# Folding the compressed keys and values from high and low parts, and a new order at the end of the cross attention

## The chip, the cores and the metric

The kernel runs on one core of one Trainium2 chip. The metric is the time of one execution on the device, in microseconds (us); several runs are timed, and one more execution is recorded by the hardware profiler. The engines are named as in the profile: PE does the matmuls (PEld loads their stationary operand), DVE is the vector engine, ACT the scalar engine, POOL the GpSimd engine, SP issues most of the DMAs. Every engine works through its own queue in order.

## The reference

The reference is one layer of a decoder trunk: 512 tokens of width 1024, 256 memory tokens. The normalized input `h` is projected once, `z = h @ W_in`, and the columns of `z` go to a pooling mixer (A), a sparse attention (B) and a cross attention into the memory (C); their gated sum goes through `w_o` and is followed by a retrieval over 16384 single-neuron experts and a last norm. What matters here is one piece of B, the compressed keys and values:

```python
cmp_start = jnp.arange(n_cmp) * CMP_STRIDE                # n_cmp = 31, stride 16
tok_idx = cmp_start[:, None] + jnp.arange(CMP_LEN)[None]  # windows of 32 tokens

def compress(tok, pe, w):                                 # tok: (B, T, 4 heads, 64)
    blk = tok[:, tok_idx] + pe[None, None, :, None, :]
    blk = blk.transpose(0, 1, 3, 2, 4).reshape(B, n_cmp, G, CMP_LEN * dh)
    return blk @ w                                        # (32*64) -> 64

kc = compress(k_cmp_tok, pe_k, w_cmp_k)
vc = compress(v_cmp_tok, pe_v, w_cmp_v)
```

`pe` is a learned encoding of the 32 places of a window. The pooling mixer takes, for its group `gr`, a trailing mean over 2, 4, 8 or 16 tokens minus the token, and then a 128x128 matrix of the group.

## The kernel before, in words

All large matmuls are made from split operands. A matrix X becomes a high part, `hi`, in the format fp32r, and a low part, `lo = X - hi`, also fp32r; a product is the sum of `hi*hi`, `lo*hi` and `hi*lo`. The helper `split` makes both parts: ACT copies the source into `hi` (line 144), then DVE (or POOL, for weights) subtracts (line 145).

A **z tile** is 128 columns of `z`, for all 512 tokens: 24 matmuls of 512 columns (line 172), 16 with the high part of the weights and 8 with the low part, into a PSUM bank of the tag `z`. There are two banks of each tag (`z`, `S`, `tr`, `o`), used in turn: a new tile takes the bank of the one before last and waits until that one's last reader is done. The weights come through `Feed`: SP fetches a raw tile `wr`, ACT makes `wh`, POOL makes `wl`. `take` hands out the tile that is due and, right behind it in the queues, has the next one split (`ahead`). So the split of the next z tile's weights stands in ACT's queue after everything that was issued before this `take`, and ahead of what is issued after it.

The stretch that the change touches is written out by hand as a list of steps, `cross_order`. Each step issues its instructions on all engines at once, in the order of the list, so the list is the order of every engine's queue:

- `Z0`..`Z3` (`cross_q`): the z tile of a cross-attention head's queries, then `qh` on ACT and `ql` on DVE.
- `S` (`cross_scores`): 12 matmuls into two banks `S`; for each, DVE takes the maximum (line 475) and ACT two exponentials (line 478).
- `R` (`cross_scale`): DVE, a reciprocal and four scalings (line 487).
- `T` (`cross_turn`): 8 transposes into two banks `tr` (line 496), each split by ACT and DVE into `xPT`.
- `O` (`cross_out`): 6 matmuls (line 508) into a bank `z`, split into `oxh`, `oxl`.
- `P` (`pool_window`): a z tile; POOL clears the margins of `u` and `pacc` (lines 523, 529), ACT copies `z` to `u` (line 524), DVE adds shifted copies (line 530, one to four times, three for `P2`, four for `P3`), forms `pl` (lines 534 to 536), and `pl` is split into `ph`.
- `G` (`pool_group`): the group's matrix on `ph` (3 matmuls into a bank `z`; `G3` comes later, into `S`), then `poolh` on ACT and `pooll` on DVE (lines 544, 545).
- `v00`..`v13` (`values`): the values of the two other branches, 24 matmuls of 280 columns into a bank `o`; ACT and DVE split 256 columns of the bank into `V` (lines 144, 145), and ACT takes the last 24 columns into `gsig` (line 439).
- `k0`, `k1`, `v0`, `v1` (`cmp_z`): a z tile of two heads' keys (values) to be compressed. Four DVE instructions (line 572), one for each head and half window, add the encoding `pe2` and write the sum into `TP`, which is f32 and is so laid out that the place within the half window is a row of its own.
- `kc`, `vc` (`cmp_fold`): 16 matmuls in plain f32 (line 580), 128 weights by 124 columns, into a bank `o`; the profile shows 32 instructions for them, two for each. `kc` is then split into `KC`, `vc` is copied into `vt` (line 587).
- `A`: has the weights of one more z tile split ahead.

Behind the list come the relative bias table (`bias_table`, line 664, `rtab` at line 665), the first z tiles of the sparse attention's keys and queries, and, after the first four chunks of four matmuls of these, `cmp_rows`: four transposes of `vt` (line 592), split into `VC` (lines 144, 145), and copies into `VH` (line 600). `G3` follows three chunks later. From there on the order of the work is as written in other parts of the kernel that the change does not touch.

Of the kernel before, what the change touches and what calls it, by code (L numbers as in the profile page):

```python
# [10 lines left out]
F32 = mybir.dt.float32  # L11
F32R = mybir.dt.float32r
# [3 lines left out]
AF = mybir.ActivationFunctionType  # L16
OP = mybir.AluOpType
# [14 lines left out]
def f(ap):  # L32
    return ap.bitcast(F32)
# [15 lines left out]
def drain(gen):  # L49
    for _ in gen:  # L50
        pass
# [70 lines left out]
def layer(ctx: ExitStack, tc: tile.TileContext, A: dict, out: bass.AP, dbg=None):  # L122
    nc = tc.nc
    v, s, g, pe = nc.vector, nc.scalar, nc.gpsimd, nc.tensor
# [6 lines left out]
    def sbuf(stack, name, side="left"):  # L131
        return stack.enter_context(tc.tile_pool(name=name, bufs=1, side=side, reuse_waits="tile"))

    def psum(tag, shape, bufs=2, dt=F32):
        return ps.tile(shape, dt, tag=tag, name=tag, bufs=bufs)
# [7 lines left out]
    def split(hi, lo, src, eng=None):  # L143
        s.activation(hi, src, AF.Copy)  # L144
        (eng or v).tensor_tensor(lo, src, f(hi), op=OP.subtract)  # L145
# [88 lines left out]
    for vc in range(2):  # L234
        for kq in range(2):
            feed.plan(("mv", vc, kq), A["w_mv"][vc, kq], 4, 256, v if vc else None)
    cross_order = ("Z0 v00 S0 v01 R0 v02 T0 v03 W1 Z1 P0 O0 S1 v10 R1 v11 T1 G0 Z2 P1 O1 S2 v12 R2 v13 T2 G1 "
                   "Z3 P2 O2 A S3 k0 R3 k1 T3 v0 G2 kc O3 v1 P3 vc G3")
    cross_order = cross_order.split()
    for c in cross_order:  # L240
        if c[0] == "Z":
# [46 lines left out]
    pm = gfeed.pool = sbuf(pms, "pm", "right")  # L288
# [103 lines left out]
    def ztile_steps(key, p):  # L392
        yield from mm3_steps(p, feed.take(key), hn, KD)

    def ztile(i):
        p = psum("z", [128, T])
        drain(ztile_steps(("z", i), p))
        return p
# [5 lines left out]
    KC = ap_.tile([128, 4, 2, 32], F32R, name="KC")  # L404
# [50 lines left out]
    def cross_q(hx):  # L455
        p = ztile(20 + hx)
        qh = xw.tile([128, T], F32R, name="qh")
        ql = xw.tile([128, T], F32R, name="ql")
        s.activation(qh, p, AF.Copy, scale=128.0 ** -0.5)
        v.scalar_tensor_tensor(ql, p, 128.0 ** -0.5, f(qh), op0=OP.mult, op1=OP.subtract)  # L460
        XQ[hx] = (qh, ql)
# [19 lines left out]
    def cross_scale(hx):  # L481
        pr, sm = XP[hx]
        v.reciprocal(sm, sm)
        for hq in range(2):
            for q_ in range(2):
                qb = 2 * hq + q_
                v.tensor_scalar(pr[:, qb], pr[:, qb], sm[:, qb:qb + 1], None, op0=OP.mult)
# [61 lines left out]
    cst = ExitStack()  # L549
    C = {}  # L550

    def cmp_open():
        cp = C["cp"] = sbuf(cst, "cp")
        for kv in range(2):
            C["wc", kv] = cp.tile([128, 16, 128], F32, tag="wc", name="wc")
            C["pe2", kv] = cp.tile([128, 2, 16], F32, tag=f"pe2{kv}", name="pe2")
            for a in (0, 64):
                for half in range(2):
                    nc.sync.dma_start(C["pe2", kv][a:a + 64, half], A["pe2"][kv, half * 64:half * 64 + 64])
            if kv == 0:  # L560
                nc.sync.dma_start(C["wc", 0], A["w_cmp"][0])

    def cmp_z(kv, gp_):
        cp = C["cp"]
        if gp_ == 0:
            C["TP", kv] = cp.tile([128, 16, 4, 31], F32, tag="TP", name="TP", bufs=2)
        p = ztile(4 + 2 * kv + gp_)
        for gi in range(2):
            a = gi * 64
            for half in range(2):  # L570
                b = half * 64
                v.tensor_tensor(C["TP", kv][b:b + 64, :, gp_ * 2 + gi],
                                p[a:a + 64, half * 16:half * 16 + 496].rearrange("p (c l) -> p l c", l=16),
                                C["pe2", kv][a:a + 64, half][:, :, None].to_broadcast([64, 16, 31]), op=OP.add)

    def cmp_fold(kv):
        cp, wc, TP = C["cp"], C["wc", kv], C["TP", kv]
        pc = psum("o", [128, 256])
        for l in range(16):
            pe.matmul(pc[:, 0:124], wc[:, l], TP[:, l], start=l == 0, stop=l == 15)  # L580
        pcv = pc[:, 0:124].rearrange("p (g c) -> p g c", c=31)
        if kv == 0:
            nc.sync.dma_start(C["wc", 1], A["w_cmp"][1])
            split(KC[:, :, 0, 0:31], KC[:, :, 1, 0:31], pcv)
        else:
            C["vt"] = pm.tile([64, 4, 31], F32, name="vt")
            v.tensor_copy(C["vt"], pcv[0:64])

    def cmp_rows():
        pt = psum("tr", [128, 4, 128])  # L590
# [14 lines left out]
    for c in cross_order:  # L605
        n = int(c[1]) if c[1:].isdigit() else None
        if c[0] == "Z":
            cross_q(n)
        elif c[0] == "S":
            cross_scores(n)  # L610
        elif c[0] == "R":
            cross_scale(n)
        elif c[0] == "W":
            wv_part(n)
        elif c[0] == "T":
            cross_turn(n)
        elif c[0] == "O":
            cross_out(n)
        elif c[0] == "P":
            pool_window(n)  # L620
            if n == 0:
                gfeed.fetch(1)
                gfeed.part(1)
        elif c == "A":
            feed.fetch(feed.i + 2)
            feed.part(feed.i + 2)
        elif c == "G3":
            pass
        elif c[0] == "G":
            pool_group(n)  # L630
        elif len(c) == 3:
            br, b = int(c[1]), int(c[2])
            values(br, b)
            if (br, b) == (1, 3):
                vst.close()
                v.tensor_scalar(gsig, gsig, 0.5, 0.5, op0=OP.mult, op1=OP.add)
                v.tensor_scalar(gsig[:, 0, 0:16], gsig[:, 0, 0:16], has, None, op0=OP.mult)
                cmp_open()
        elif c == "kc":
            cmp_fold(0)  # L640
        elif c == "vc":
            cmp_fold(1)
        else:
            cmp_z(int(c[0] == "v"), n)
    cst.close()
    xwst.close()
    dump("poolT", f(poolh)); dump("poolL", f(pooll))
# [401 lines left out]
    for at in attention():  # L1049
# [5 lines left out]
        while done < goal:  # L1055
            c = next(filler, None)
# [68 lines left out]
    src = A["iota128"]  # L1125
# [178 lines left out]
    for hp in range(16):  # L1304
        if hp < 15:
            p = psum("z", [128, T])
# [515 lines left out]
def _layout(I):  # L1822
    a = {}
    a["x"] = I["x"][0]
    a["mem"] = I["mem"][0]
    a["rel_bias"] = I["rel_bias"]
    for k in ("g_mix", "g_mem", "g_ffn"):
        a[k] = I[k][0]
    a["g_final"] = I["g_final"]
    w = I["w_in"][0]  # L1830
    o_q, o_kv, o_g, o_x, o_m = 512, 1536, 3072, 3120, 3632
    kvc = [w[:, o_kv + 256 * i:o_kv + 256 * (i + 1)] for i in range(6)]
    q = w[:, o_q:o_kv]
    ks = np.stack([kvc[2].reshape(D, 4, 64), kvc[4].reshape(D, 4, 64)], axis=2).reshape(D, 512)
    zt = np.concatenate([ks, kvc[0], kvc[1], q, w[:, 0:512], w[:, o_x:o_m], w[:, o_m:]], axis=1)
    a["w_z"] = _tiles(zt, 128)
    wv = []
    for i, vv in enumerate((kvc[3], kvc[5])):
        wv.append(_tiles(np.concatenate([vv, w[:, o_g + 24 * i:o_g + 24 * (i + 1)]], axis=1), 280)[0])
    a["w_v"] = np.stack(wv)  # L1840
    wc, pe = [], []
    for kk in ("k", "v"):
        w4 = I["w_cmp_" + kk][0].reshape(2, 16, 64, 64)
        one = w4.transpose(0, 2, 1, 3).reshape(128, 16, 64)
        wc.append(np.concatenate([one, one], axis=2))
        pe.append(I["pe_" + kk][0].reshape(2, 16, 64).transpose(0, 2, 1).reshape(128, 16))
    a["w_cmp"] = np.stack(wc)
    a["pe2"] = np.stack(pe)
    a["w_pool_grp"] = I["w_pool_grp"][0]
    a["pool_scale"] = I["pool_scale"][0].reshape(4, 128).T  # L1850
    a["w_pool_out"] = _tiles(I["w_pool_out"][0], 128)
    a["w_nsa_out"] = _tiles(I["w_nsa_out"][0], 128)
    a["w_x_out"] = _tiles(I["w_x_out"][0], 128)
    mk = I["w_mem_kv"][0]
    a["w_mk"] = _tiles(mk[:, 0:512], 128)
    a["w_mv"] = mk[:, 512:].reshape(2, 4, 128, 2, 256).transpose(3, 0, 2, 1, 4).reshape(2, 2, 128, 1024)
    a["w_o"] = I["w_o"][0].reshape(4, 2, 128, 2, 512).transpose(3, 0, 2, 1, 4).reshape(2, 4, 128, 1024)
    a["w_peer_q"] = _tiles(I["w_peer_q"][0], 128)
    a["sub_keys"] = I["peer_sub_keys"][0].reshape(16, 128, 128).transpose(2, 0, 1)
    u4 = I["peer_u"][0].reshape(128, 128, D)  # L1860
    a["u_t"] = u4.reshape(128, 128, KD, 128).transpose(1, 3, 2, 0).reshape(128, 128, KD * 128)
    a["u_rows"] = u4.transpose(1, 0, 2).reshape(128 * 128, D)
    a["v_rows"] = I["peer_v"][0].reshape(128, 128, D).transpose(1, 0, 2).reshape(128 * 128, D)
    a = {k: np.ascontiguousarray(x) for k, x in a.items()}
    a.update(_consts())
    return a
# [15 lines left out]
```

## Time and profile before

| | |
|---|---|
| median of 3 runs | 1793.06 us (1792.14 to 1795.39) |
| the profiled execution, its own time | 1791.84 us |
| its span, first to last instruction | 1790.1 us |
| PE busy | 1769.6 us, 99% of the span |
| DVE, ACT, POOL busy | 1374.7, 832.8, 855.8 us |
| share of PE in the chain that ended last | 90% |
| the steps `Z3` to `vc` in the trace | from 103.6 to 154.7 us |

The page's busy times say how much of the span an engine had an instruction at work. The chain is followed back from the last instruction, at each step to what released it; its times in order show where PE works without a gap and where another engine holds the end. In a list in order of time, a row has the start, the duration, the engine, the line, the operation, what is written from what, and in brackets how long the engine had been idle and what ended that.

### The profile page before, as it was taken

What the parts mean: (1) busy time and instruction counts of PE and PEld (TensorE: products, weight loads), DVE (VectorE), ACT (ScalarE), POOL (GpSimd) and SP (SyncE); (2) the same over time, 40 slices, a digit from 0 to 9 for tenths busy, and PEclk for the clock granted to TensorE, in tenths of its full rate; (3) what the DMA queues carried; (4) which work ended last, traced back from release to release, by engine and by line L of the source; (5) the groups of instructions that cost most, each with busy time, mean ns of one, the idle gap of its engine ahead of it and who ended that gap; (6) DMA issues with size and microseconds to landing.
All of it is one profiled execution on the core that took longest, in us unless ns stands there. A gap on an engine that the chain in (4) does not pass through costs nothing.

```text
span 1790.1 us, 28200 instructions
## 1 busy us (share of the span) xinstructions
PE 1769.6 (99%) x10114; PEld 1564.2 (87%) x10114; DVE 1374.7 (77%) x2846; ACT 832.8 (47%) x1476; POOL 855.8 (48%) x681
## 2 busy tenths in 40 slices
PE   8999999999999999999999999999999999999998
PEld 7988888888888888999999999999999988888886
DVE  5454147776653369999999976999998999999997
ACT  6434257777642333463555554333333333333334
POOL 3333555556643323434555405666666654444430
PEclk9999999999999999999999999999999999999999
DMA  6225631112123532377999989999999999999993
GB/s 227 90 85 163 218 122 60 49 60 71 60 77 99 187 125 83 114 244 239 360 362 372 374 293 388 410 409 391 381 395 384 366 390 406 408 406 403 398 407 127
DMA packets 155614, 456.55 MB, mean 255 GB/s; under 512 B 16513, under 2 KB 55857, under 8 KB 152786
## 3 DMA queue, kind: packets, MB, share of 16 engines
q1 hardware_dynamic: 80850, 253.10, 38.9%
q0 software_dynamic: 47488, 172.38, 25.0%
q10 hardware_dynamic: 27136, 29.26, 4.9%
q8 instruction: 80, 1.31, 0.3%
q14 instruction: 60, 0.49, 0.1%
HBM read 411.82 MB, written 48.10 MB: 257 GB/s over the span
## 4 chain that ended last, share of the span: by engine, by line
PE 90%; DVE 4%; ACT 3%; DMA 1%; issue 1%; POOL 0%; DVEq 0%; SPq 0%; ACTq 0%; POOLq 0%
PE z L172 47%; PE S L1656 9%; PE tr L1656 9%; PE o L1656 9%; PE S L916 2%; PE tr L948 1%; PE o L964 1%; PE S L1177 1%; PE o L435 1%; PE o L1497 1%; PE S L1497 1%; PE tr L1497 1%; PE o L1261 1%; ACT pr L929 1%; DVE wl L145 0%
## 5 line engine op out<-in xcount | busy, mean ns | idle before, releaser
L144 ACT ACTIVATE wh<-wr 128x1024 fp32r<-128x1024 f32 (+2 forms) x365 | 371.4, 1025 | 140.7 <-PE z L172 45.2
L145 POOL TENSOR_TENSOR wl<-wr,wh 128x1024 fp32r<-128x1024 f32 (+2 forms) x110 | 241.8, 2199 | 320.1 <-ACT wh L144 267.9
L172 PE MATMUL z<-hfh,wh 128*128 128x336 f32 (+1 forms) x1136 | 362.6, 326 | 0.1
L172 PE MATMUL z<-hfl,wh 128*128 128x336 f32 (+1 forms) x1136 | 359.4, 323 | 0.0
L145 DVE TENSOR_TENSOR wl<-wr,wh 128x1024 fp32r<-128x1024 f32 x255 | 306.2, 1216 | 58.4 <-ACT wh L144 56.9
L1520 POOL DMA_INDIRECT ug<-in_v_rows_dram,ids x128 | 178.8, 1397 | 173.4 <-DVE x1g L1540 155.1
L1520 POOL DMA_INDIRECT ug<-in_u_rows_dram,ids x128 | 199.8, 1561 | 92.0 <-DVE ug L1534 74.1
L172 PEld LDWEIGHTS z<-hfh,wh 128*128 128x128 f32 x1136 | 213.3, 188 | 7.6 <-ACT wh L144 1.0
L172 PEld LDWEIGHTS z<-hfl,wh 128*128 128x128 f32 x1136 | 213.4, 188 | 6.5
L172 PE MATMUL z<-hfh,wl 128*128 128x336 f32 (+1 forms) x1136 | 207.1, 324 | 1.1 <-DVE wl L145 1.1
L144 ACT ACTIVATE wgh<-gh 128x384 fp32r<-128x384 f32 x128 | 67.3, 526 | 286.8 <-DVE gh L1635 273.5
L172 PEld LDWEIGHTS z<-hfh,wl 128*128 128x128 f32 x1136 | 182.3, 188 | 7.6 <-DVE wl L145 1.9
L1226 ACT ACTIVATE hg<-z 128x336 f32<-128x336 f32 x128 | 57.7, 451 | 232.8 <-PE z L172 232.6
L1540 DVE SCALAR_TENSOR_TENSOR x1g<-ug,wgt,x1g 128x1024 f32<-128x1024 f32 x128 | 163.9, 1280 | 1.4
L1534 DVE SCALAR_TENSOR_TENSOR ug<-ug,hf 128x1024 f32<-128x1024 f32 x128 | 152.4, 1218 | 5.7 <-DMA ug<-in_u_rows_dram,ids 5.7
L172 PE MATMUL z<-hnh,wh 128*128 128x512 f32 x384 | 150.8, 393 | 0.0
L172 PE MATMUL z<-hnl,wh 128*128 128x512 f32 x384 | 150.2, 391 | 0.0
L1420 POOL DMA_INDIRECT ux<-in_u_rows_dram,idx x48 | 89.6, 1866 | 53.9 <-DVE ux L1428 48.8
L937 POOL TENSOR_SCALAR pr<-pr,sm,gsig 128x128 f32<-128x128 f32 (+3 forms) x128 | 78.5, 617 | 74.6 <-DVE sm L1011 58.3
L952 DVE TENSOR_TENSOR PB<-tr,PB 128x128 fp32r<-128x128 f32 (+3 forms) x128 | 62.5, 488 | 50.5 <-ACT PB L951 50.1
L172 PE MATMUL z<-hnh,wl 128*128 128x512 f32 x384 | 98.8, 392 | 0.0
L145 DVE TENSOR_TENSOR wgl<-gh,wgh 128x384 fp32r<-128x384 f32 x128 | 71.1, 556 | 32.8 <-ACT wgh L144 32.8
(418 smaller groups left out, 3651.1 us busy)
## 6 DMA issues: line engine op xcount, KB each, us to landing
wr<-in_u_t_dram SPq DMA_DIRECT2D x128, 512.0 KB, 6.7
wr<-in_v_rows_dram SPq DMA_DIRECT2D x128, 512.0 KB, 9.8
wr<-in_w_z_dram SPq DMA_DIRECT2D x48, 512.0 KB, 3.6
gd<-stg ACTq DMA_DIRECT2D x11, 2048.0 KB, 16.9
hg<-hd SPq DMA_DIRECT2D x80, 168.0 KB, 10.9
gj<-gd SPq DMA_DIRECT2D x8, 1408.0 KB, 12.5
go<-gd SPq DMA_DIRECT2D x8, 1408.0 KB, 15.1
hd<-hg POOLq DMA_DIRECT2D x66, 168.0 KB, 6.3
```

The source lines that it names most:

```text
L144: s.activation(hi, src, AF.Copy)
L145: (eng or v).tensor_tensor(lo, src, f(hi), op=OP.subtract)
L172: pe.matmul(p, w[a][:, k], xs(x[b], k), start=k == 0 and a == 0 and b == 0, stop=k == nk - 1 and a == 1)
L937: g.tensor_scalar(pr[:, 0:n], pr[:, 0:n], sm, gsig[:, qb, c:c + 1], op0=OP.mult, op1=OP.mult)
L952: return lambda: v.tensor_tensor(lo, pt[:, 0:qb + 1], f(hi), op=OP.subtract)
L1226: s.activation(hg[:, X:], p[:, X:NT], AF.Gelu)
L1420: g.indirect_dma_start(out=XR[k], out_offset=None, in_=A["u_rows"], in_offset=bass.IndirectOffsetOnAxis(ap=idx[:, k:k + 1], axis=0))
L1497: pe.matmul(pg[:, n], oa[:, t_ // 2, :, t_ % 2], ob[:, r, t_ // 2, :, t_ % 2], start=n == 0 and r == 0, stop=n == 3 and r == 1, skip_group ...
L1520: g.indirect_dma_start(out=row, out_offset=None, in_=src, in_offset=bass.IndirectOffsetOnAxis(ap=ids[:, b, k:k + 1], axis=0))
L1534: v.scalar_tensor_tensor(row, row, 1.0, hf[:, b], op0=OP.mult, op1=OP.mult, accum_out=act[:, m:m + 1])
L1540: v.scalar_tensor_tensor(X1[b], rows.pop(m), wgt[:, m - 128:m - 127], X1[b], op0=OP.mult, op1=OP.add)
L1656: pe.matmul(acc_o[2 * b + half], a[:, b * 128:(b + 1) * 128], c[:, half], start=k == 0 and i == 0, stop=k == 127 and i == 2)
```

## The change

Three things are changed, all in this stretch.

The fold is made from parts. The weights `w_cmp` are no longer stored twice side by side; `cmp_load` fetches 64 columns, and `cmp_weights` splits them (ACT, and POOL for the low part) into `wcs`, whose 128 columns are the 64 high and the 64 low ones. `cmp_parts` takes the place of the four additions: it splits the four pieces of the z tile, so that there is an ACT copy and a DVE subtraction for each, into `TP`, now fp32r with 250 columns: 124 high, 124 low, and two more, the encoding's high and low part. So one chain of 16 matmuls of 250 columns yields all products, in two halves of 64 partitions. `cmp_fold` sums them: ACT copies the lower half into `low`, DVE adds the encoding's columns, copies one, and makes two sums of 124 columns into `t_`. For the keys, `KC` is then made of `t_` by two copies on ACT and two subtractions on DVE.

The encoding `pe2` comes in two DMAs in place of eight. The second weights are loaded after `k1` in place of after `kc`, and there is one buffer of `TP` in place of two.

The order is changed: `P2` moves from behind `Z3` to behind `k1`; `k0` comes ahead of `S3`; `kc` moves from behind `G2` to ahead of `v0`.

```diff
-    cross_order = (... "Z3 P2 O2 A S3 k0 R3 k1 T3 v0 G2 kc O3 v1 P3 vc G3")
+    cross_order = (... "Z3 O2 A k0 S3 R3 k1 P2 T3 kc v0 G2 O3 v1 P3 vc G3")

+    def cmp_load(kv):
+        C["raw", kv] = C["cp"].tile([128, 16, 64], F32, name="wc")
+        nc.sync.dma_start(C["raw", kv], A["w_cmp"][kv])
+
+    def cmp_weights(kv):
+        C["wc", kv] = C["cp"].tile([128, 16, 2, 64], F32R, name="wcs")
+        split(C["wc", kv][:, :, 0], C["wc", kv][:, :, 1], C["raw", kv], g)

     def cmp_open():
...
+            C["pe2", kv] = cp.tile([128, 16], F32, tag=f"pe2{kv}", name="pe2")
+            nc.sync.dma_start(C["pe2", kv], A["pe2"][kv])
+        cmp_load(0)

     def cmp_z(kv, gp_):
...
+        C["p", kv, gp_] = ztile(4 + 2 * kv + gp_)
+
+    def cmp_parts(kv, gp_):
+        if gp_ == 0:
+            TP = C["TP", kv] = C["cp"].tile([128, 16, 250], F32R, name="TP")
+            split(TP[:, :, 248], TP[:, :, 249], C["pe2", kv])
+        p, TP = C.pop(("p", kv, gp_)), C["TP", kv]
         for gi in range(2):
+            src = p[gi * 64:gi * 64 + 64]
+            o = (gp_ * 2 + gi) * 31
             for half in range(2):
                 b = half * 64
-                v.tensor_tensor(C["TP", kv][b:b + 64, :, gp_ * 2 + gi], ..., op=OP.add)
+                split(TP[b:b + 64, :, o:o + 31], TP[b:b + 64, :, 124 + o:155 + o],
+                      src[:, half * 16:half * 16 + 496].rearrange("p (c l) -> p l c", l=16))

     def cmp_fold(kv):
...
         for l in range(16):
-            pe.matmul(pc[:, 0:124], wc[:, l], TP[:, l], start=l == 0, stop=l == 15)
+            pe.matmul(pc[:, 0:250], wc[:, l].rearrange("p r d -> p (r d)"), TP[:, l], ...)
+        t_ = pm.tile([64, 4, 31], F32, name="vt")
+        tf = t_.rearrange("p g c -> p (g c)")
+        low = C["cp"].tile([64, 250], F32, name="low")
+        s.activation(low, pc[64:128, 0:250], AF.Copy)
+        v.tensor_tensor(low[:, 248:250], low[:, 248:250], pc[0:64, 248:250], op=OP.add)
+        v.tensor_copy(low[:, 249:250], pc[0:64, 249:250])
+        for i in range(2):
+            v.scalar_tensor_tensor(tf, pc[0:64, i * 124:i * 124 + 124], low[:, 248 + i:249 + i],
+                                   tf if i else low[:, 0:124], op0=OP.add, op1=OP.add)
         if kv == 0:
-            nc.sync.dma_start(C["wc", 1], A["w_cmp"][1])
-            split(KC[:, :, 0, 0:31], KC[:, :, 1, 0:31], pcv)
+            for a in (0, 64):
+                s.activation(KC[a:a + 64, :, 0, 0:31], t_, AF.Copy)
+            for a in (0, 64):
+                v.tensor_tensor(KC[a:a + 64, :, 1, 0:31], t_, f(KC)[0:64, :, 0, 0:31], op=OP.subtract)
         else:
-            C["vt"] = pm.tile([64, 4, 31], F32, name="vt")
-            v.tensor_copy(C["vt"], pcv[0:64])
+            C["vt"] = t_

     # in the loop over cross_order
             cmp_z(int(c[0] == "v"), n)
+            cmp_parts(int(c[0] == "v"), n)
+            if n == 0:
+                cmp_weights(int(c[0] == "v"))
+            if c == "k1":
+                cmp_load(1)
```

More of the change, by code (lines that the diff above doesn't have):

```diff
@@ L237, in layer @@
     cross_order = ("Z0 v00 S0 v01 R0 v02 T0 v03 W1 Z1 P0 O0 S1 v10 R1 v11 T1 G0 Z2 P1 O1 S2 v12 R2 v13 T2 G1 "
-                   "Z3 P2 O2 A S3 k0 R3 k1 T3 v0 G2 kc O3 v1 P3 vc G3")
+                   "Z3 O2 A k0 S3 R3 k1 P2 T3 kc v0 G2 O3 v1 P3 vc G3")
     cross_order = cross_order.split()
@@ L554, in cmp_open @@
         for kv in range(2):
[L555 to L561, printed above, removed]
+            C["pe2", kv] = cp.tile([128, 16], F32, tag=f"pe2{kv}", name="pe2")
@@ L563, in cmp_z @@
+            nc.sync.dma_start(C["pe2", kv], A["pe2"][kv])
+        cmp_load(0)
     def cmp_z(kv, gp_):
-        cp = C["cp"]
+        C["p", kv, gp_] = ztile(4 + 2 * kv + gp_)
+    def cmp_parts(kv, gp_):
         if gp_ == 0:
-            C["TP", kv] = cp.tile([128, 16, 4, 31], F32, tag="TP", name="TP", bufs=2)
-        p = ztile(4 + 2 * kv + gp_)
+            TP = C["TP", kv] = C["cp"].tile([128, 16, 250], F32R, name="TP")
+            split(TP[:, :, 248], TP[:, :, 249], C["pe2", kv])
+        p, TP = C.pop(("p", kv, gp_)), C["TP", kv]
@@ L568, in cmp_z @@
         for gi in range(2):
-            a = gi * 64
+            src = p[gi * 64:gi * 64 + 64]
+            o = (gp_ * 2 + gi) * 31
             for half in range(2):
                 b = half * 64
-                v.tensor_tensor(C["TP", kv][b:b + 64, :, gp_ * 2 + gi],
-                                p[a:a + 64, half * 16:half * 16 + 496].rearrange("p (c l) -> p l c", l=16),
-                                C["pe2", kv][a:a + 64, half][:, :, None].to_broadcast([64, 16, 31]), op=OP.add)
+                split(TP[b:b + 64, :, o:o + 31], TP[b:b + 64, :, 124 + o:155 + o],
+                      src[:, half * 16:half * 16 + 496].rearrange("p (c l) -> p l c", l=16))
@@ L576, in cmp_fold @@
     def cmp_fold(kv):
-        cp, wc, TP = C["cp"], C["wc", kv], C["TP", kv]
+        wc, TP = C["wc", kv], C["TP", kv]
         pc = psum("o", [128, 256])
         for l in range(16):
-            pe.matmul(pc[:, 0:124], wc[:, l], TP[:, l], start=l == 0, stop=l == 15)
-        pcv = pc[:, 0:124].rearrange("p (g c) -> p g c", c=31)
+            pe.matmul(pc[:, 0:250], wc[:, l].rearrange("p r d -> p (r d)"), TP[:, l], start=l == 0, stop=l == 15)
+        t_ = pm.tile([64, 4, 31], F32, name="vt")
@@ L1844, in _layout @@
         one = w4.transpose(0, 2, 1, 3).reshape(128, 16, 64)
-        wc.append(np.concatenate([one, one], axis=2))
+        wc.append(one)
         pe.append(I["pe_" + kk][0].reshape(2, 16, 64).transpose(0, 2, 1).reshape(128, 16))
```

## The prediction

> **What bounds the kernel now.** I read the page first, then the windows of the stretch that the change touches, then the chain that ended last in order of time.
>
> ```profile
> PE 1769.6 (99%) x10114; PEld 1564.2 (87%) x10114; DVE 1374.7 (77%) x2846; ACT 832.8 (47%) x1476; POOL 855.8 (48%) x681
> PE 90%; DVE 4%; ACT 3%; DMA 1%; issue 1%; POOL 0%; DVEq 0%; SPq 0%; ACTq 0%; POOLq 0%
> ```
> ```profile
> 103.00:163.00 60.00, 60.00 (x307) 50.09 (x306) 30.56 (x56) 20.01 (x42) 21.34 (x22) 1.00 0.28 88
> 163.00:222.00 59.00, 59.00 (x262) 48.88 (x261) 8.23 (x12) 22.51 (x32) 29.04 (x25) 1.00 0.72 234
> ```
> ```profile
> 115.98 1.41 PE S L473 x12
> 117.39 10.90 PE z L172 x48
> 128.29 0.87 PE tr L496 x8
> 129.16 6.14 PE z L172 x27
> 135.31 3.57 PE o L580 x32
> 138.88 1.38 PE z L508 x6
> 140.25 10.89 PE z L172 x48
> 151.14 3.57 PE o L580 x32
> 154.71 0.96 PE z L664 x2
> 155.67 3.86 PE z L172 x16
> 159.53 0.34 PE tr L592 x4
> ```
>
> PE is never idle from 103 to 222 us (first number of the windows: length, then PE, PEld, DVE, ACT, POOL busy). So whatever PE saves in the steps up to `vc` comes off the end, and whatever idle time is put between its steps is added: the 59 us behind, gapless too, absorb nothing. ACT is busy 20 of 60 us and DVE 31, but in order; what counts is when, after a z tile, each of them is done with it.
>
> **Part 1: the matmuls of the fold.** 32 instructions take 3.57 us a fold. In their place stand 16 fp32r matmuls of 250 columns. The nearest row are the 12 score matmuls of 256 columns, 1.41 us, 0.1175 each: 16 x 0.1175 = 1.88 us, a gain of 1.69 a fold, **3.4 us** in all. That is also the most that the change can gain. From the other side: fp32r with few columns might run at a quarter of the rate.
>
> ```profile
> L812 PE MATMUL z<-KC,Q x64: 192/277/278, 222.3 to 423.6; 128*128 128x64 f32 x64
> L473 PE MATMUL S<-Kh,qh x16: 279/279/279, 48.6 to 116.9; 128*128 128x256 f32 x16
> ```
>
> 64 columns take as long (277 ns) as 256 (279), which would fit that, at 16 x 0.43 = 6.9 us a fold. But the quickest takes 192 ns, 85 less: one whose weights were loaded before its turn. The others wait for weights, not for columns. I take 1.88.
>
> **Part 2: the splitting, and what orders it.** Before, a z tile to be compressed costs four DVE additions, 2.8 us. Now each piece is an ACT copy and a DVE subtraction, all eight reading one PSUM bank. Does ACT's second copy wait for DVE's first subtraction, though neither needs the other's result? The trace has three places with two engines on one bank.
>
> ```profile
> 100.82 0.42 DVE L145 TENSOR_TENSOR V<-o,V 128x256 fp32r<-128x256 f32 x1 [1.74 <-ACT V L144]
> 101.28 0.19 ACT L439 ACTIVATE gsig<-o 128x24 f32<-128x24 f32 x1 [0.49 <-DVE V L145]
> 160.15 0.21 DVE L145 TENSOR_TENSOR VC<-tr,VC 31x64 fp32r<-31x64 f32 x1 [1.88 <-ACT VC L144]
> 160.39 0.21 ACT L144 ACTIVATE VC<-tr 31x64 fp32r<-31x64 f32 x1 [0.28 <-DVE VC L145]
> 160.64 0.21 DVE L145 TENSOR_TENSOR VC<-tr,VC 31x64 fp32r<-31x64 f32 x1 [0.28 <-ACT VC L144]
> 169.24 1.20 ACT L744 ACTIVATE Q<-z 64x512 fp32r<-64x512 f32 x2
> 170.47 1.39 DVE L749 SCALAR_TENSOR_TENSOR Q<-z,Q 64x512 fp32r<-64x512 f32 x2 [3.35 <-ACT Q L744]
> ```
>
> `gsig` reads other columns of the bank than DVE's subtraction does and needs nothing from it, yet starts 0.04 us after its end. The four splits of `VC` out of one bank go strictly in turn, 0.49 us each for two instructions of 0.21. And the first subtraction of `Q` needs only the first copy (partitions 0 to 63), but starts 0.03 after the second (partitions 64 to 127) ended. So accesses of two engines to one PSUM tile stand in the program's order here, whichever part they read. The change issues copy, subtraction, copy, subtraction, where `Q` issues both copies first.
>
> ```profile
> 163.88 0.57 ACT L716 ACTIVATE KK<-z 64x512 fp32r<-64x512 f32 x1
> L572 DVE TENSOR_TENSOR TP<-z,pe x16: 666/673/679, 122.9 to 147.8; 64x496 f32<-64x496 f32 x16
> ```
>
> One turn is 0.58 + 0.04 + 0.67 + 0.04 = 1.33 us; four, begun 0.2 after the tile's end, are done **5.5 us** after it (without that order 3.6: copies 0.5 apart, subtractions 0.7), and both ACT and DVE are held for that long. Encoding columns (0.2 on each engine) and `cmp_weights` (ACT 1.05, POOL 2.4) ride along.
>
> **Part 3: the new order, walked through.** Durations not shown yet:
>
> ```profile
> 109.91 0.69 DVE L460 SCALAR_TENSOR_TENSOR ql<-z,qh 128x512 fp32r<-128x512 f32 x1 [4.31 <-ACT qh L459]
> 121.41 0.47 ACT L478 ACTIVATE xpr<-S,xnm 128x256 f32<-128x256 f32 x1 [0.52 <-DVE xnm L475]
> 120.70 1.28 DVE L475 TENSOR_REDUCE xnm<-S 128x2 f32<-128x512 f32 x2
> 123.23 1.07 ACT L144 ACTIVATE wh<-wr 128x1024 fp32r<-128x1024 f32 x1
> 124.38 2.40 POOL L145 TENSOR_TENSOR wl<-wr,wh 128x1024 fp32r<-128x1024 f32 x1 [1.00 <-ACT wh L144]
> 114.74 0.60 ACT L524 ACTIVATE u<-z 128x512 f32<-128x512 f32 x1 [3.92 <-PE z L172]
> 118.82 0.63 ACT L144 ACTIVATE ph<-pl 128x512 fp32r<-128x512 f32 x1 [3.48 <-DVE pl L536]
> 128.76 1.09 ACT L144 ACTIVATE xPT<-tr 128x512 fp32r<-128x512 f32 x2 [4.47 <-PE tr L496]
> 134.66 2.78 DVE L572 TENSOR_TENSOR TP<-z,pe 64x496 f32<-64x496 f32 x4 [2.28 <-PE z L172]
> 137.47 0.75 DVE L545 SCALAR_TENSOR_TENSOR pooll<-z,scl,poolh 128x512 fp32r<-128x512 f32 x1
> 157.39 0.28 DVE L587 COPY vt<-o 64x124 f32<-64x124 f32 x1
> ```
>
> `k0` needs `Z3`'s bank; `qh` (0.60, as `u`) and `ql` free it 1.65 us after `Z3` with their hand-overs, and only `O2`, 1.36, lies between: **0.3** idle. Now count from `k0`'s end. `k0`'s turns hold DVE to 5.5, the maxima of `S3` follow to 6.8, its four exponentials (0.47 each) to 8.1, and only then comes `wh` for `P2` in ACT's queue: ready at 9.2. PE has had `S3` (1.41) and `k1` (5.45) and wants `P2` at 6.9: **2.4** idle. `P2` ends at 14.7. `k1`'s turns run on ACT from 9.05 to 13.6, then `wh` for `v0`, and POOL's `wl` to 17.1; the clearing of `u` stands behind that, so ACT's `u` starts at 17.3 in place of 14.9. From `u` to `ph` the trace has 4.1 us: `ph` at 21.4, and the copies for `T3` behind it to 23.0, `low` of `kc` to 23.3, four DVE additions behind DVE's part of `T3` to 24.9, `KC` to 25.5, `wh` for `v1` to 26.5, the encoding 0.2: only at 26.7 do `v0`'s turns begin, done at 32.0. PE meanwhile: `T3` 0.87, `kc` 1.88, `v0` 5.45, `G2` 0.68, at 23.6. `O3` takes the bank of the z tile before last, `v0`'s, and must wait for its last subtraction: **8.5** idle. Before, `kc` stood between, 3.57 us of cover, and the bank was free at 137.44, ahead of `O3` at 138.88.
>
> Smaller ones: `v1` needs `G2`'s bank, whose `poolh` (0.7) and `pooll` (0.75) now come behind `v0`'s turns, 0.6. `vc` needs `v1`'s turns (5.5, cover `P3` 5.45), 0.2. Behind `v1`'s turns stand `wh` and `wl` of the next weights, (ACT free 0.7 ahead of `P3`'s end, then 1.05 and 2.4), so `u` of `P3` starts 3.0 after `P3`'s end, not 0.2; the first key tile needs that bank, 0.7. Then `vt`: `u` at 3.0, 4.9 to `ph` (one addition more than `P2`), 0.63 and 0.69 for its split with `low` beside it, and the sums, two as long as `vt`'s copy and two narrow ones, 1.0 as an estimate: 10.3 after `P3`. PE reaches line 592 after `vc`, the bias table, and 3.64 of the key tile, 7.3 after `P3`: **3.1** idle. Before, `vt` was one copy, at 157.7, 1.8 ahead.
>
> **Part 4: PE's clock after the long gap.**
>
> ```profile
> 7.50 1.97 PE L203 MATMUL tr<-ident,hb 128*128 128x128 f32 x8 [1.38 <-DVE hb L324]
> 14.22 1.27 PE L203 MATMUL tr<-ident,hb 128*128 128x128 f32 x8
> 1775.00:1790.00 15.00, 8.14 (x35) 6.14 (x34) 9.85 (x20) 5.79 (x17) 0.00 (x0) 0.86 0.29 106
> ```
>
> The first 16 transposes, over some 3.4 us from 7.5, go at about half the pace of those at 14.2, and in the last 15 us, where PE idles, the granted clock is 0.86 (the number ahead of the last two). After 8.5 us of idleness I expect `O3` and a little of `v1` at half pace: at most 1.7, at least nothing; 0.6 is covered by `v1`'s own wait. I take 1.2.
>
> **At nothing** I put the DMAs: two of `pe2` in place of eight, a smaller `w_cmp` fetched some 20 us ahead; the second one waits on SP for POOL's low part of the first, done 8.3 after `k0`, ahead of the next fetch; uncovered, it would hold up the fetch for `v1`, wanted at 25.5. `G2` finds `ph` ready 0.1 early.
>
> **The sum.** Idle 0.3 + 2.4 + 8.5 + 0.6 + 0.2 + 0.7 + 3.1 = 15.8, less 3.4, plus 1.2: **+13.6** on the profiled execution's 1791.84 us. The median of the runs is 1793.06, 1.2 above it, so 1806.7; the chained waits lean to the long side, and I say **1806 us**.
>
> **Rivals.** *(a) Order only within a half of the partitions.* Then the third copy runs beside the second subtraction, a z tile is done 0.67 sooner, and four such steps on the way leave 2.5 less: 1804. Against it stands the `Q` row. The Trainium skill, "PSUM — Partial Sum Buffer", section "PSUM bank collisions raise a hardware error", states that two engines collide, reads included, only in the same bank and the same quadrant of 32 partitions; that rule asks for the order within a half and would let the halves overlap, so by it the time is this rival's, while the trace's `Q` copies are ordered more coarsely.
>
> *(b) No order within the bank at all; not slower.* Copies run ahead and a z tile is done at 3.6. The waits are then 0.3, 0.4, 4.2 (`O3`) and 1.4 (line 592), 6.3 less 3.4: +2.9, 1796, within what a measurement of this kernel can tell from no change (0.2%, 3.6 us). Only the reading of `gsig` and `VC` as something else would save it. *(c) ACT also reaches `v0`'s copies in time.* The four DVE instructions alone still end 3.0 after the tile's end, 2.3 after `G2`; with every other wait gone that is 3.4 - 2.3, 1792. Faster decides itself at `O3`: its bank must be free under 4 us after `v0`'s end.
>
> *(d) The fold doesn't get quicker*, 6.9 us each by Part 1's other bound: `kc`'s excess is mostly hidden in `O3`'s wait and `vc`'s in that of line 592; about 2.8 more, 1809.
>
> **How the numbers follow.** Forecast 0.62 (its own range 1802 to 1810), (a) 0.12, (b) 0.11, (c) 0.08, (d) 0.07. Range 1796 to 1811: it reaches to (b), leaves out (c) and some tails. Slower by over 0.2%: forecast, (a), (d) and the upper half of (b), 0.83 with a little off for a forecast much too long; within 0.2%: 0.13; faster: 0.04, the tail of (c).
>
> **What would show it.** In the profile after: 16 matmuls at line 580's successor in about 1.9 us; ACT's copies into `TP` 1.33 apart, each ended in its wait by DVE; PE idle ahead of `O3` by 8 us, ahead of `P2` and the transposes of `vt` by 2 to 3; 0.3 ahead of `k0`. Copies 0.5 apart would make it (b); a gap before `O3` under 3 us, (c); folds of 7 us, (d). I am wrong most easily in `O3`'s wait, a sum of ten queued steps.

## The result, and the profile after

The changed kernel takes **1810.66 us** (median of 6 runs, 1808.85 to 1811.35) against 1792.96 before (6 runs, 1792.14 to 1795.39): ratio 1.0098, 95% interval 1.0088 to 1.0108. That is 17.7 us lost; the forecast was 13 (1806, range 1796 to 1811). The profiled execution took 1810.61 us, with a span of 1808.7.

From the page: busy times of the engines, then the chain that ended last.

```profile
PE 1771.7 (98%) x10082; PEld 1562.8 (86%) x10082; DVE 1383.0 (76%) x2856; ACT 846.4 (47%) x1499; POOL 857.7 (47%) x683
PE 87%; DVE 6%; ACT 3%; DMA 2%; issue 1%; POOL 1%; SPq 0%; DVEq 0%; ACTq 0%; POOLq 0%
```

PE has 32 matmuls fewer and is yet busy 2.1 us longer; its share of the chain falls from 90% to 87%, and DVE's rises from 4% to 6%. The two windows of the prediction show where (length, PE, PEld, DVE, ACT, POOL busy, then the granted clock):

```profile
103.00:163.00 60.00, 46.80 (x214) 37.87 (x213) 30.30 (x49) 25.84 (x49) 20.18 (x14) 0.91 0.22 63
163.00:222.00 59.00, 56.57 (x249) 45.57 (x248) 15.62 (x30) 24.60 (x41) 24.18 (x25) 0.97 0.58 192
```

Of 119 us that were gapless before, PE is idle for 15.6, and the granted clock, 1.00 before in both, is 0.91 and 0.97. The waits of PE from 103 to 182 us (in total, times, longest; hand-overs of up to 0.3 us are not counted in this view):

```profile
PE z L508 <- DVE TP L145: 10.3, 1, 10.3
PE tr L609 <- DVE vt L596: 2.4, 1, 2.4
PE z L172 <- ACT wh L144: 2.2, 1, 2.2
PE o L588 <- DVE TP L145: 0.6, 1, 0.6
```

These are `O3`, the transposes of `vt`, `P2` and `kc`. The chain that ended last, in order of time (start, length, engine and work), shows what stands behind the first of them. Before, it was PE alone in this stretch; now it leaves PE at the end of `k0` and comes back 35 us later:

```profile
111.44 5.79 PE z L172 x24
117.25 0.60 ACT TP L144
117.88 0.68 DVE TP L145
118.58 0.60 ACT TP L144
119.20 0.68 DVE TP L145
...
125.52 3.33 DVE xpr L487 x4
...
145.12 2.90 DVE TP L145 x2
...
151.32 0.69 DVE TP L145
152.14 2.90 PE z L508 x6
```

The turns are there, 1.33 us apart, ACT's third copy (it reads partitions 64 to 127) waiting for DVE's second subtraction (partitions 0 to 63). Two rows are far too long: four scalings of `R3` take 3.33 us, where before they took 1.8, with one of the four at 1.0, and the chain holds DVE for 2.90 at 145.12, where the encoding's 128x16 subtraction and the first piece should need 0.9. Both are taken up below.

### The profile page after: what moved, and what is told of

Read it like the earlier page. It is cut to its first block, busy times and chain, and to the rows that moved or that the text cites. A ratio compares the mean times of both kernels' runs of the same rounds, so it can differ in the third digit from the quotient of the medians.

```text
span 1808.7 us, 28158 instructions
## 1 busy us (share of the span) xinstructions
PE 1771.7 (98%) x10082; PEld 1562.8 (86%) x10082; DVE 1383.0 (76%) x2856; ACT 846.4 (47%) x1499; POOL 857.7 (47%) x683
## 4 chain that ended last, share of the span: by engine, by line
PE 87%; DVE 6%; ACT 3%; DMA 2%; issue 1%; POOL 1%; SPq 0%; DVEq 0%; ACTq 0%; POOLq 0%
PE z L172 45%; PE S L1678 9%; PE tr L1678 9%; PE o L1678 9%; PE S L938 2%; PE tr L970 1%; PE o L986 1%; PE S L1199 1%; PE o L435 1%; POOL wl L145 1%; PE o L1519 1%; PE S L1519 1%; PE tr L1519 1%; ACT wh L144 1%; PE o L1283 1%
```

## The experiments

All are timed against the kernel before in the same session (its medians there: 1792.2, 1792.74, 1793.06 and 1792.87 us).

| run | median us | ratio to before, 95% |
|---|---|---|
| after | 1810.66 | 1.0098 [1.0088, 1.0108] |
| order_alone | 1797.38 | 1.0025 [1.0016, 1.0035] |
| parts_alone | 1808.79 | 1.0091 [1.0074, 1.0108] |
| copies_first | 1805.12 | 1.0070 [1.0053, 1.0087] |
| via_sbuf | 1809.62 | 1.0096 [1.0080, 1.0113] |
| enc_last | 1808.92 | 1.0093 [1.0078, 1.0109] |
| warm | 1809.10 | 1.0094 [1.0078, 1.0109] |
| covered | 1796.88 | 1.0024 [1.0014, 1.0034] |
| covered2 | 1791.45 | 0.9991 [0.9982, 1.0000] |
| covered_turns | 1793.09 | 1.0001 [0.9992, 1.0010] |
| covered3 | 1790.37 | 0.9984 [0.9975, 0.9993] |

**Which half of the change costs?** First the order alone, in the kernel before:

```diff
-                   "Z3 P2 O2 A S3 k0 R3 k1 T3 v0 G2 kc O3 v1 P3 vc G3")
+                   "Z3 O2 A k0 S3 R3 k1 P2 T3 kc v0 G2 O3 v1 P3 vc G3")
```

> The kernel before with the new order of the steps and nothing else. Theory (two engines on one PSUM tile take turns in program order, so the split of a z tile holds ACT, DVE and the bank): the order alone costs only the two waits that the old additions leave, 0.3 us ahead of k0 and 2.4 us ahead of O3, at most 1.7 more if PE's clock drops: 1795.7 to 1797.4 us. Rival (the order itself is what costs, since kc no longer stands ahead of O3 and P2 no longer ahead of S3): most of the 17.7 us stay, 1805 us or more.

It lost 5.2 us. The waits of PE from 103 to 185 us are one row:

```profile
PE z L508 <- DVE TP L572: 2.3, 1, 2.3
```

That is `O3` again, for `v0`'s bank. With 0.3 ahead of `k0`, 2.7 us of the loss are these waits. At 164 us this profiled run is 3.5 us behind that of before, 0.5 of it from ahead of the stretch, and at 1600 us still 3.8; 1.7 more comes between 1680 and 1700 us, 0.7 of it in waits of PE for split weights, and its cause is open. Its ten runs spread over 4.3 us. The granted clock stayed at 1.00 through the stretch, so the 1.7 us that the expectation allowed for it did not come; that the time still reaches the upper end of the expected range is owed to the late loss, and is luck.

Then the rest of the change alone, in the order of before:

```diff
-                   "Z3 O2 A k0 S3 R3 k1 P2 T3 kc v0 G2 O3 v1 P3 vc G3")
+                   "Z3 P2 O2 A S3 k0 R3 k1 T3 v0 G2 kc O3 v1 P3 vc G3")
```

> The changed kernel with the order of before: new fold, new splitting, old list. Theory: the turns still hold ACT and DVE for 5.5 us after each z tile; the same walk through the queues gives waits of 1.6 us ahead of T3, 5.1 ahead of kc, 0.9 in small ones and 3.1 ahead of the transposes of vt, less 3.2 for the folds, plus 1.5 to 4 for the clock: 1802 to 1805 us. Rival (the order costs): the fold's gain is left alone, 1789.8 us.

16.6 us lost, more than either reading gave. The two halves don't add up (5.2 and 16.6 against 17.7): with the new parts, the new order adds only about 1. The wait of 5.1 expected ahead of `kc` came, at 5.6, ahead of `O3`. Two things make up the excess: the wait ahead of `T3`, expected at 1.6, is 4.9, and half rate lay on 11.2 us of matmuls, which cost 5.6 where at most 4 was expected. PE's largest waits, then DVE's and POOL's own rows in the same stretch:

```profile
PE z L508 <- DVE TP L145: 5.6, 1, 5.6
PE tr L496 <- DVE xpr L487: 4.9, 3, 2.0
```
```profile
129.50 5.33 DVE L487 TENSOR_SCALAR xpr<-xpr,xsm 128x256 f32<-128x256 f32 x4
```
```profile
129.73 2.35 POOL L145 TENSOR_TENSOR wcs<-wc,wcs 128x1024 fp32r<-128x1024 f32 x1 [5.69 <-ACT wcs L144]
132.03 2.39 POOL L145 TENSOR_TENSOR wl<-wr,wh 128x1024 fp32r<-128x1024 f32 x1
```

Four scalings of 256 columns (SBUF in, SBUF out) take 5.33 us: the second and the third, 2.45 and 2.43, each last until one of POOL's two subtractions has ended; the first and the last take 0.35. `T3` waits for them one by one.

**The turns.** ACT's four copies ahead of DVE's four subtractions, nothing else:

```diff
-                split(TP[b:b + 64, :, o:o + 31], TP[b:b + 64, :, 124 + o:155 + o],
-                      src[:, half * 16:half * 16 + 496].rearrange("p (c l) -> p l c", l=16))
+                pieces.append((TP[b:b + 64, :, o:o + 31], TP[b:b + 64, :, 124 + o:155 + o],
+                               src[:, half * 16:half * 16 + 496].rearrange("p (c l) -> p l c", l=16)))
+        for hi, lo, src in pieces:
+            s.activation(hi, src, AF.Copy)
+        for hi, lo, src in pieces:
+            v.tensor_tensor(lo, src, f(hi), op=OP.subtract)
```

> The changed kernel with the four ACT copies of a z tile issued ahead of the four DVE subtractions, the same instructions otherwise. Theory: DVE's first subtraction waits for the fourth copy, a z tile is done 5.0 us after its end instead of 5.5, but ACT is free after 2.2 instead of 4.8 us and the next weights are split sooner: O3's wait falls from 10.5 to about 6, the wait of the vt transposes to about 1.5, 1802 to 1804.5 us. Rival (the order of the steps, or the port that DVE and POOL share, makes the waits): no change, 1809 to 1811 us.

5.5 us less than the changed kernel, or 4.8 when each is set against the kernel before in its own session, and 0.6 above the expected range. Two of PE's waits:

```profile
PE z L508 <- DVE TP L587: 5.9, 1, 5.9
PE tr L614 <- DVE vt L601: 0.4, 1, 0.4
```

The wait ahead of `O3` is 5.9 in place of 10.3, that of `vt` 0.4 in place of 2.4. Against this, a half-rate stretch that the changed kernel doesn't have fell on `P2` and cost 1.5 (its windows are shown below). The turns are some 30% of the loss, and without that stretch would be more.

**The bank given back early.** ACT copies the z tile into SBUF once, and both parts are made from that:

```diff
         p, TP = C.pop(("p", kv, gp_)), C["TP", kv]
+        zc = C["cp"].tile([128, T], F32, name="zc")
+        s.activation(zc, p, AF.Copy)
+        p = zc
```

> The changed kernel with one more ACT instruction, a copy of the whole z tile from PSUM to SBUF; the four splits read that copy, so the bank is free 0.8 us after ACT begins and copies and subtractions need not take turns. Theory (the PSUM tile's turns are the cost): ACT's copies 0.5 us apart, waits of about 2 us ahead of O3, 3.4 ahead of v1 (poolh of G2 stands behind the copies) and 2 ahead of the vt transposes: 1798 to 1802 us. Rival (DVE instructions whose operands all lie in SBUF are held while POOL subtracts, as the 0.17 us subtraction of the encoding was held for 2.3 us): the subtractions take over 1 us each and the time stays above 1803 us.

Hardly less than the changed kernel. PE's waits, and two groups on `TP` (shortest, median and longest ns):

```profile
PE z L172 <- DVE pooll L545: 5.3, 1, 5.3
PE z L172 <- ACT wh L144: 3.1, 1, 3.1
PE tr L612 <- DVE vt L599: 2.1, 1, 2.1
PE z L508 <- ACT zc L577: 1.1, 1, 1.1
```
```profile
L144 ACT ACTIVATE TP<-zc x16: 1034/1075/1130, 117.8 to 164.3; 64x496 fp32r<-64x496 f32 x16
L145 DVE TENSOR_TENSOR TP<-zc,TP x16: 974/1010/1071, 119.0 to 165.4; 64x496 fp32r<-64x496 f32 x16
```

`O3` does get its bank (1.1), but `v1` then waits 5.3 for `G2`'s, whose `poolh` stands behind the same copies on ACT. And the pieces got slower: 1.08 and 1.01 us out of SBUF against 0.59 and 0.67 out of PSUM. That the subtractions take over 1 us is the rival's figure, but not its cause: none of the 16 was held; the only one that began inside one of POOL's did so 0.04 us before that ended. Freeing the bank moved the wait by one step, to the queue of ACT and DVE; how much of the 5.3 the slower pieces made, this run does not separate.

**Why an instruction of 16 columns takes 2.3 us.** The encoding's split behind the four pieces:

```diff
-            split(TP[:, :, 248], TP[:, :, 249], C["pe2", kv])
...
+        if gp_ == 0:
+            split(TP[:, :, 248], TP[:, :, 249], C["pe2", kv])
```

> The changed kernel, but the split of the encoding column stands behind the four pieces of the z tile, not ahead of them. Nothing is left out. Theory (VectorE waits for GpSimd: an instruction with all its operands in SBUF is held while GpSimd subtracts the low part of a weight): the 128x16 subtraction, 2.31 us in the changed kernel and ahead of the four pieces of v0, then falls outside that subtraction and takes about 0.2; the wait ahead of O3 falls from 10.5 to about 8.4 us, the median to 1807 to 1809.3 (the half clock behind the wait can be a stretch of 3.4 us shorter or not). Rival (the 2.3 us belong to that instruction itself, its stride of 250 columns): it takes 2.3 us at the new place too, the wait stays at 10.3 to 10.5 and the median within 1 us of the changed kernel's 1810.7.

The changed kernel's rows of DVE and POOL ahead of `v0`'s pieces, then the same subtraction as a group in this run:

```profile
145.12 2.31 DVE L145 TENSOR_TENSOR TP<-pe,TP 128x16 fp32r<-128x16 f32 x1 [0.96 <-ACT TP L144]
```
```profile
145.05 2.34 POOL L145 TENSOR_TENSOR wl<-wr,wh 128x1024 fp32r<-128x1024 f32 x1 [7.04 <-ACT wh L144]
```
```profile
L145 DVE TENSOR_TENSOR TP<-pe,TP x2: 193/193/193, 121.9 to 149.8; 128x16 fp32r<-128x16 f32 x2
```

Begun 0.07 us after POOL, it ended with POOL, in both places of the changed kernel; away from POOL's subtraction it takes 0.19. `O3`'s wait, with its hand-over, fell by 2.5 us to 8.0, the time by 1.7 (part of the gain went to a half-rate stretch that now fell on `P2`, below). So the instruction isn't slow, it is held. In `R3` of the changed kernel the same is read from the trace (three scalings of 0.35 and one of 2.53 that ends 0.15 after POOL's subtraction); no run moved these out of POOL's way. The subtractions that read PSUM are not held. In copies_first three of `k0`'s four overlap a subtraction of POOL's, and all four take 0.67 to 0.68; nor is a reciprocal of four columns held, with its one input in SBUF, which the kernel before has inside POOL's subtraction of 124.38 to 126.77:

```profile
118.89 2.73 DVE L587 TENSOR_TENSOR TP<-z,TP 64x496 fp32r<-64x496 f32 x4 [4.25 <-ACT TP L585]
```
```profile
120.02 2.40 POOL L145 TENSOR_TENSOR wcs<-wc,wcs 128x1024 fp32r<-128x1024 f32 x1 [5.43 <-ACT wcs L144]
```
```profile
125.69 0.18 DVE L483 RECIPROCAL xsm<-xsm 128x4 f32<-128x4 f32 x1
```

So what stretches to POOL's end are this subtraction with both inputs in SBUF, and the scalings. The other way round, POOL waits too: in via_sbuf its subtraction at 133.04, begun beside one of DVE's out of SBUF, took 2.88 us in place of 2.4. This fits the Trainium skill, "SBUF — State Buffer", section "Who interferes with whom": VectorE and GpSimd share a port pair that the first to issue holds for its whole instruction, and a VectorE instruction with two SBUF inputs, or in a two-port mode, needs it. That the scalings ran in such a mode, no run here shows.

**The clock.** Matmuls that compute nothing, in the two longest waits:

```diff
+    def warm(k):
+        pw = psum("S", [128, T])
+        for i in range(k):
+            pe.matmul(pw, hnh[:, 0, 0:128], hnh[:, 0], start=i == 0, stop=i == k - 1)
...
+            if n == 3:
+                warm(40)
             cross_out(n)
...
+            warm(9)
             cmp_rows()
```

> The changed kernel with matmuls put in that compute nothing: 40 of 512 columns ahead of O3 (some 9.1 us) and 9 ahead of the transposes of vt (some 2.0 us), both within the waits that are there. Theory (TensorE's idleness brings the half clock): no half-rate stretch behind O3's wait and behind that of vt; O3 takes 1.36 us instead of 2.73, v1 with P3 10.9 instead of 11.8, the 12 matmuls behind the transposes 2.85 instead of 4.46; 3.5 to 4 us less than the changed kernel's 1810.7, 1806.5 to 1807.5, with the waits' ends where they were. Rival (the half rate has another cause, or the wait's own length decides whatever runs in it): the same slow matmuls, within 0.8 us of 1810.7 or above it.

The same stretch of the changed kernel (behind `O3`'s wait), and of this one (granted clock: third number from the right):

```profile
152.00:155.50 3.50, 3.36 (x8) 2.71 (x9) 0.75 (x1) 1.68 (x4) 2.80 (x2) 0.50 0.01 2
```
```profile
152.00:155.50 3.50, 3.15 (x13) 2.29 (x14) 1.44 (x2) 2.52 (x5) 3.16 (x3) 1.00 0.01 2
```

No half rate is left; `O3` takes 1.47 us instead of 2.73, the 12 matmuls behind the transposes 2.89 instead of 4.46, `v1` with `P3` 11.0 instead of 11.8. So idleness brings the half rate, and it cost 3.6 us at these three places. The time fell by only 1.6, though, and stayed 1.6 above the expected range: `v1` now waits 0.5 us for `G2`'s bank and the third key and query tile 0.8 for its own, waits that the slow matmuls had hidden.

Which gaps count? In the traces' record of the clock, the half-rate stretches ahead of the last 20 us of a run last 3.413, 6.827 or 10.24 us, multiples of 3.413. Cut into windows of that length on the same grid, three runs show (the window with the gap, then the one behind it):

```profile
122.60:126.01 3.41, 1.47 (x7) 0.89 (x5) 1.91 (x5) 2.97 (x10) 2.36 (x1) 1.00 0.02 5
126.01:129.42 3.41, 3.14 (x14) 2.59 (x15) 3.41 (x4) 0.68 (x2) 2.40 (x1) 1.00 0.49 154
173.80:177.21 3.41, 1.14 (x7) 0.92 (x8) 2.39 (x7) 2.24 (x5) 1.48 (x1) 1.00 0.00 0
177.21:180.62 3.41, 3.41 (x9) 2.65 (x8) 0.65 (x3) 1.67 (x7) 0.89 (x1) 0.50 0.72 238
```
```profile
123.78:127.19 3.41, 1.38 (x6) 1.16 (x7) 2.31 (x5) 2.44 (x8) 2.34 (x2) 1.00 0.40 111
127.19:130.61 3.42, 3.42 (x10) 2.63 (x9) 2.43 (x3) 0.89 (x2) 1.03 (x1) 0.50 0.40 113
```
```profile
121.84:125.26 3.42, 1.45 (x7) 0.87 (x5) 1.92 (x6) 2.83 (x10) 0.58 (x1) 1.00 0.46 150
125.26:128.67 3.41, 3.31 (x8) 2.63 (x9) 3.40 (x4) 3.34 (x6) 2.36 (x1) 0.50 0.02 8
```

(After, enc_last, copies_first.) A window in which PE was busy for 1.14, 1.38 or 1.45 us is followed by one at half rate; one with 1.47 was not (the gap of 2.37 us ahead of `P2`). In the other traces no window contradicts this: at full rate, 1.36 us or less came ahead of half rate, and 1.62 or more ahead of full. So in these runs a gap of 2.2 to 2.6 us costs another 1.6 or nothing, by where it falls. The Trainium skill, "TensorE: Matmul & The Clock Gate", section "What's actually happening", states the free-running window of 3413 ns; it asks for an idle window, where here one busy for a third was enough.

**A placement that covers the parts.** If the loss is all in queues, the folds' gain must come back once every tile's parts have something to hide behind. These lines differ from the changed kernel (the two of `feed` have the weights of the tile after next split ahead of a tile's parts; `pg` gives `G2` a bank `S`); beside them, the copies stand ahead of the subtractions and the encoding's split behind them, as in copies_first and enc_last:

```diff
+                   "Z3 O2 S3 R3 k0 T3 k1 P2 O3 A kc v0 G2 v1 P3 vc G3")
...
-        pg = psum("z" if gr < 3 else "S", [128, T])
+        pg = psum("z" if gr < 2 else "S", [128, T])
...
             cmp_z(int(c[0] == "v"), n)
+            feed.fetch(feed.i + 2)
+            feed.part(feed.i + 2)
...
-        if n == 3:
+        if n == 6:
             cmp_rows()
-        if n == 6:
+        if n == 8:
             pool_group(3)
```

> The folds of the change, with cover for every z tile's parts: the four ScalarE copies ahead of the four subtractions, the encoding's split behind them, the weights of the tile after next split ahead of a tile's parts, the order Z3 O2 S3 R3 k0 T3 k1 P2 O3 A kc v0 G2 v1 P3 vc, G2 on an S bank, the turned values and the last group's matmuls two or three steps later. Nothing is left out. Theory (the loss is all in waits for the parts, in the order of the queues, and in the clock behind them; the fold itself gains 3.2 us): by the queue walk one wait of 0.3 is left, no half clock, 1789 to 1791, at least 2 us below before. Rival (the parts cost something that no placement hides, such as banks or SBUF traffic that slow the matmuls, or the walk overlooks a wait): some wait of 2 us or more is left, 1793 or above.

1796.88, the rival's case by its numbers: a miss. One wait, with 3.4 us of half rate behind it, took more than the gain. From 103 to 165.7 us PE has no gap above 0.1; then:

```profile
PE z L172 <- DVE KK L751: 4.5, 1, 4.5
```
```profile
162.81 1.06 ACT L144 ACTIVATE wh<-wr 128x1024 fp32r<-128x1024 f32 x1 [5.44 <-DMA wr<-in_w_z_dram]
163.90 0.59 ACT L746 ACTIVATE KK<-z 64x512 fp32r<-64x512 f32 x1
...
166.09 1.27 ACT L623 ACTIVATE VH<-VC 32x128 fp32r<-32x128 f32 x4
167.37 0.59 ACT L746 ACTIVATE KK<-z 64x512 fp32r<-64x512 f32 x1
```

My own delay of `cmp_rows` put the turned values and four copies into `VH` between the first key tile's two copies. With `cmp_rows` at step 4, `pool_group(3)` back at 6, and the copies into `VH` at step 16:

> The kernel covered, in which one wait of 4.64 us was left ahead of the third key and query tile: there ScalarE had the turned values and their four copies into VH to do ahead of the first key tile's copies. Here the turned values stand two steps earlier (one step later than in the changed kernel), the four copies into VH twelve steps later, and the last group's matmuls where they were. Nothing is left out. Theory (that wait is only the place of these instructions in ScalarE's queue; the rest of the parts is hidden): no wait above 0.6 us from 103 to 200 us, no half clock, 1790 to 1791.7, below before by 1 to 2.5 us. Rival (the wait belongs to the stretch, whatever stands in the queue): 3 us or more of waiting elsewhere, 1794 or above.

As the theory had it, except for one wait of 1.3 left at the same place (1.49 with its hand-over). In the rows above, ACT had sat for a DMA until 162.81 (in covered2 until 162.85); SP's own queue in covered2 shows why:

```profile
158.50 0.31 SPq L694 DMA_DIRECT2D scr<-rtab  x1
158.92 1.36 SPq L87 DMA_DIRECT2D wr<-in_w_z_dram  x2
```

One line, the fetch ahead of the bias table, is covered3:

```diff
+    feed.fetch(feed.i + 3)
     bias_table()
```

> The kernel covered2 with one line more: the third key and query tile's weights are fetched ahead of the bias table, not behind it. In covered2's trace that fetch stands in SyncE's queue behind the store of the bias table, which waits for VectorE until 158.5 us; it goes out at 158.9, lands at 162.8, and ScalarE's split of these weights waits for it ahead of the first key tile's copies; TensorE then waits 1.49 us at 165.7. Nothing is left out. Theory (that queue is the cause): the split starts by 161, the wait falls to under 0.3 us, 1789.6 to 1790.8, below before by 1.5 to 3.5 us. Rival (the wait is one of the bank, set by the copies themselves): 1.0 to 1.5 us left and covered2's time, 1791.4, within 0.5.

1790.37 us, **2.5 below the kernel before** (ratio 0.9984, 0.9975 to 0.9993). PE waits for nothing from 103 to 222 us, and the chain is PE alone again, with the new folds in it:

```profile
103.00:163.00 60.00, 60.00 (x288) 48.88 (x287) 37.32 (x69) 34.79 (x65) 27.80 (x25) 1.00 0.27 85
```
```profile
131.44 1.86 PE o L594 x16
...
150.34 1.99 PE o L594 x16
```

**Do the turns matter under cover?** covered2 with copy and subtraction in turn again:

> The kernel covered2 with the pieces in the change's turns again (copy, subtraction, copy, subtraction). Nothing is left out. Theory (the turns make a z tile's parts 0.4 us longer, and hold ScalarE 2.9 us longer; with cover most of it is hidden): the queue walk leaves a wait of about 1.5 us ahead of O3 and one of 1.6 ahead of vc, 3 us above covered2, 1793 to 1795. Rival (the turns cost what copies_first won against the changed kernel, whatever the cover): 5 us or more above covered2.

```profile
PE o L589 <- DVE TP L145: 1.4, 1, 1.4
PE z L508 <- ACT u L524: 1.0, 1, 1.0
```

The two waits came where they were expected, at 1.2 (expected 1.5) ahead of `O3` and 1.6 ahead of `vc`, with hand-overs; the time is 1.6 above covered2, not 3, because covered2's own 1.49 us wait shrank to 0.3 behind them. Under cover the turns cost 1.6, in the changed kernel about 5.

## Why the prediction was right, and where it was not

Sign, mechanism and most terms held; the size held only just. 1810.66 lies above the forecast's own range (1802 to 1810) and 0.3 under the end of the whole one (1811), which is partly luck: the two terms below were too small by 4.7 us together, `kc` was put at 0 and cost 0.7, and errors the other way gave back 1.9. Term by term, predicted and measured in the profiled run (gaps with their hand-overs):

| step | predicted | measured |
|---|---|---|
| two folds | -3.4 | -3.2 (1.98 us each) |
| ahead of `k0` | 0.3 | 0.28 |
| ahead of `P2` | 2.4 | 2.37 |
| ahead of `kc` | 0 | 0.72 |
| ahead of `O3` | 8.5 | 10.49 |
| `v1`, `vc`, first key tile | 0.6, 0.2, 0.7 | 0, 0.09, 0 more than before |
| ahead of `vt`'s transposes | 3.1 | 2.59 |
| half clock | 1.2 | 3.9 |
| sum | +13.6 | +17.2 |

The two profiled executions are 18.8 us apart (1810.61 and 1791.84), more than the medians. At 93 us, ahead of the stretch, the changed one was later by 0.8 already; from there to 182 us it lost 17.5, of which the table has 17.2, and some 0.5 behind.

Two terms were mis-sized. **Part 4, the clock**: I charged it behind `O3` only, and bounded it by 1.7. It was 1.37 in `O3` and 0.87 behind it (half rate until 156.7 us, 4.6 us of work), and 1.61 behind the transposes of `vt`, a gap of 2.6 us that I had charged nothing for. That second place was a matter of phase; `P2`'s similar gap got off free. **Part 3, `O3`'s wait**: `v0`'s turns began at 145.1, not the 143.75 that the walk gives, and took 6.9 us, not 5.3. The walk gave DVE's small instructions their free-standing durations. `k1`'s first copy came at 126.1, as the walk had it, but its subtraction, due at 126.7, began at 128.77, behind `R3`'s scalings (3.33): `k1`'s parts were done 2 us later than in the walk, and 1.4 of that was left where `v0`'s turns began; the encoding's subtraction took 2.31 for 0.19. The trace of before held a hint, one of `R3`'s four scalings at 1.015 us beside 0.345, which the prediction does not take up.

Smaller errors went the other way. `v1`'s 0.6 was hidden by `O3`'s slow matmuls, as warm shows, where it reappears as 0.5. The step that has ACT's `u` start at 17.3, behind POOL's clearing, was wrong: `u` did not wait for the clearing, DVE's first addition did (2.94 us, until POOL's `wl` and the clearing behind it were through), so the chain to `ph` was late by less.

The rivals: *(a)* fails in this program, as the third copy waits for the second subtraction in other partitions; the order is that of the program's waits, and whether the chip would allow the overlap was not tried. *(b)* and *(c)* fall with the turns and with `O3`'s 10.5. *(d)* falls with folds of 1.98 us. The order, the other half of the change, is no culprit: it costs 2.7 us of waits with the old parts, and the old order with the new parts is nearly as slow as the new one (16.6 us lost, against 17.7).

## What to carry to other kernels

When work moves from TensorE to ScalarE and VectorE, count how long each z tile holds both of them, and put a tile of TensorE's work that long behind it; saving 3 us of matmuls paid only after the order, the bank of `G2`, the split of weights ahead and one fetch were placed for it (changed together; which of them could be spared was not tried). A wait freed at one bank turned up at the next (`O3` to `v1`, `vt` to the third key tile), so walk on past the first cure. Charge each gap of more than 2 us for the clock behind it as well.

## What was not expected of the hardware

- A VectorE subtraction with both inputs in SBUF, or a scaling out of SBUF, begun while GpSimd subtracts 128x1024, ends with it: 2.31 us for 16 columns (0.19 alone), 5.33 for four scalings beside two such subtractions (an estimate without them is 1.2, from scalings of 0.35 that start 0.27 apart). Subtractions with an input in PSUM kept their 0.67 to 0.68 beside it.
- The half clock came behind windows of 3.413 us in which TensorE was busy for up to 1.45 us, and not behind one with 1.47 or more: a gap of 2.2 us was enough in copies_first.
- Pieces of 64x496 read with a stride of 16 elements cost ScalarE 1.08 us out of SBUF and 0.59 out of PSUM; VectorE 1.01 and 0.67.
